# First weights by row block, first squares on GpSimd, a weave's weight and the last scalings: four edits to a two-layer hybrid decoder trunk

## The chip, the cores and the metric

The kernel runs on one core of a Trainium2 chip. The metric is the device time of one launch in microseconds; the median of three runs is the time of a kernel. The engines are named as in the profile: PE is TensorE's matmul side, PEld its weight loads, DVE is VectorE, ACT is ScalarE, POOL is GpSimd, SP is SyncE, which issues the transfers.

## What is computed

Two layers of a decoder, 512 tokens of width 1024, float32, and a closing RMSNorm:

```python
def _layer(x, mem, positions, ...):
    h = _rmsnorm(x, norm_g)
    p = _split_columns(h @ w_in)              # queries, keys, values, gates of all branches
    y_a = _dsa_attention(...)                 # five branches: A sparse, B forgetting (fox),
    y_b = _fox_attention(...)                 # C stick-breaking, D native sparse, E memory
    ...
    merge = jax.nn.sigmoid(p['merge'].reshape(B, S, N_BRANCH, D_MODEL))
    merged = jnp.sum(merge * jnp.einsum('bsnc,ncd->bsnd', ys, w_branch), axis=2)
    return x + merged @ w_out

def reference(x, mem, ...):
    for l in range(2):
        x = _layer(x, ...)
    return _rmsnorm(x, final_norm)
```

## The kernel before

Everything is held transposed: width on the partitions in 8 tiles of 128 rows (index `k`), the 512 tokens along the columns. A weight or an activation is split in a high part, a rounded copy made on ACT, and a low part, the rest, made by a subtraction on DVE; a product is then three matmuls (`mm3`: high by high, high by low, low by high). Weights come in blocks of 128 by 1024 floats: a transfer into one of two buffers `raw`, then a split into one of three `whi` and three `wlo` buffers. Small tiles share 28 slots of 128 by 512 floats (`slot`). PSUM has three banks `pj`, two `S` and three `T`.

The program is written in one order; a scheduler gives each engine its own fixed order from it, by the order of the program and its own estimates of time. Each engine then runs its order strictly and waits where an operand is not there.

**The start.** `begin_layer` and `begin_tile` take the 8 tiles of x: a scaled high part `u` (ACT), the square `sq` (ACT), the low part `ul` (DVE) and the running sum of the squares (DVE). In layer 0 the helper `inorder` chains these instructions on ACT and on DVE in the order in which they are written, and `start_split` puts the splits of the first weights, of `sb_q` and `sb_k` of head pair 0, among them. These weights come in two blocks of 512 KB: the first holds all 8 row tiles of `sb_q`, the second all 8 of `sb_k`. `first` then runs 8 times 2 times 3 matmuls into two banks (`k` outside, query or key inside), sums the squares over the partitions by matmuls with a column of ones (`sumsq`), takes the inverse root on DVE (`rsqrt4`, twelve tiny instructions), spreads it by a transpose (`rowb`), and meanwhile makes the values of `sb_v` from `u` and `ul`. With the spread row `rb`, `norm` makes the normalised activations `h` that every later projection reads.

**The weaves.** `weave` runs several generators in turn: each has a count that grows by 1/n at each step, and the one with the lowest count goes next (at equal counts, the one listed first). The last weave of a layer runs the forgetting attention, 16 steps with n = 16 and a tail behind the last, with the 8 steps of merging branch A, `merge(0, ...)`, n = 8. Behind it `merge(1, ...)` merges branch B, whose operand `yhi`, `ylo` comes out of that tail (inverse sums, `head_rows`, `g`, `y`, split). A merge step is a projection of 24 matmuls from `h` and 6 matmuls from a branch's output.

**The end.** `final` works in two halves of 256 tokens. For each of 8 tiles: 24 matmuls, a residual add (`xn`) on DVE, a square on ACT, an add on DVE. Then `sumsq`, `rsqrt4`, `rowb`, and 8 scalings `o` on DVE straight from PSUM, a store issued from SP for each two of them.

Of the kernel before, what the change touches and what calls it, by code (L numbers as in the profile page):

```python
# [103 lines left out]
def _layout(x, mem, positions, norm_g, w_in, kv_norm, w_uk, w_uv, fox_bias, nsa_pe_k, nsa_pe_v,  # L104
# [6 lines left out]
    for l in range(L):  # L111
        w3 = w_in[l].reshape(KT, 128, -1)

        def cols(idx):
            o = np.zeros((KT, 128, 128), f)
            ok = idx >= 0
            o[:, :, ok] = w3[:, :, idx[ok]]
            return o.transpose(1, 0, 2)

        for a, b in PAIRS:  # L120
            wall[l, CH[a]].reshape(128, 2, KT, 128)[:, 0] = cols(tl[a])
            wall[l, CH[a]].reshape(128, 2, KT, 128)[:, 1] = cols(tl[b])
        for n in VTOK:
# [63 lines left out]
def trunk(ctx: ExitStack, tc: tile.TileContext, xt, memt, pos, wall, small, vec, ca, cb, out):  # L187
# [26 lines left out]

    nc.scalar.preload_act_table_set("exp_and_others")
    xs = big.tile([128, KT, T], F32, name="x0", tag="xa")
    posi = slot("posi", I32)
    VEC = const.tile([128, V_N], F32, name="VEC")
    nc.sync.dma_start(VEC, vec)
    START_W = (1, 3)  # L220
    start_w = []
    for k in range(KT):
        nc.sync.dma_start(xs[:, k], xt[:, k])
        if k in START_W:
            r = wts.tile([128, 1024], F32, name="wraw", tag="raw", bufs=2)
            nc.sync.dma_start(r, wall[0, CH[('sb_q', 0)], :, 1024 * len(start_w):1024 * len(start_w) + 1024])
            start_w.append(r)
    CA = const.tile([128, 896], F32, name="CA")
# [8 lines left out]
    def vcol(c, n=1):  # L237
        return VEC[:, c:c + n]
# [427 lines left out]
    def begin_layer(l):  # L666

        U = [wk.tile([128, 2, T], F32R, name="u", tag=t, bufs=2) for t in ("yhi", "yhi", "ylo", "ylo", "Z", "Z")]
        u = [x[:, e] for x in U for e in range(2)]
        return SimpleNamespace(uh=u[:KT], ul=u[KT:] + [slot("ul", F32R) for _ in range(2 * KT - len(u))], sq=[])  # L670

    def begin_tile(b, l, k, x, inorder=lambda e, ins: ins, middle=lambda k: None):

        sq = slot("sq")
        g = vcol(l * V_L + V_NG + k)
        inorder(0, nc.scalar.activation(b.uh[k], x, AF.Copy, scale=g))
        middle(k)
        inorder(0, nc.scalar.activation(sq, x, AF.Square))
        inorder(1, nc.vector.scalar_tensor_tensor(b.ul[k], x, g, f32(b.uh[k]), op0=OP.mult, op1=OP.subtract))
        if k == 0 or (l and k == KT - 1):  # L680
            b.sq.append(sq)
        else:
            inorder(1, nc.vector.tensor_add(b.sq[0], b.sq[0], sq))

    def layer(l, xs, begin):
# [3 lines left out]
        def first():  # L689
# [4 lines left out]
            if l == 0:  # L694
                prev = {}

                def inorder(e, ins):
                    after(ins, prev.get(e))
                    prev[e] = ins

                def start_split(k):
                    if k in START_W:
                        w = [wts.tile([128, 1024], F32R, name="w", tag=t, bufs=3) for t in ("whi", "wlo")]
                        r = start_w[START_W.index(k)]
                        inorder(0, nc.scalar.activation(w[0], r, AF.Copy))
                        inorder(1, nc.vector.tensor_sub(w[1], r, f32(w[0])))
                        ws.append(w)

                for k in range(KT):
                    begin_tile(b, 0, k, xs[:, k], inorder, start_split)  # L710
                state['start'] = prev[0], prev[1]
            else:
                ws += [wload(l, ('sb_q', 0), 0), wload(l, ('sb_q', 0), 1)]
            uh, ul = b.uh, b.ul
            for k in range(KT):
                for a in range(2):
                    c = slice(128 * k, 128 * k + 128)
                    mm3(p[a], ws[a][0][:, c], ws[a][1][:, c], uh[k], ul[k], k == 0, k == KT - 1)
            y = rsqrt4(sumsq(b.sq, 4), D, 4)
# [590 lines left out]
        def final():  # L1310
# [25 lines left out]
            for half in range(2):  # L1336
                ts = slice(H * half, H * half + H)

                def tiles():
                    for m in range(KT):  # L1340
# [11 lines left out]
                        for k in range(KT):  # L1352
                            c = slice(128 * k, 128 * k + 128)
                            mm3(p, W[m][0][:, c], W[m][1][:, c], lv.g[k][0][:, ts], lv.g[k][1][:, ts], k == 0, k == KT - 1)
                        nc.vector.scalar_tensor_tensor(xn[:, m, ts], p, 0.25, residual(m)[:, ts], op0=OP.mult, op1=OP.add)
                        yield xn[:, m, ts]

                ssq = sumsq(squares(tiles(), True), 2)
                rb = rowb(rsqrt4(ssq, D, 2), 2)
                for j in range(KT // 2):  # L1360
                    o = slot("o", shape=(128, 2, H))
                    for e in range(2):
                        k = 2 * j + e
                        nc.vector.scalar_tensor_tensor(o[:, e], xn[:, k, ts], vcol(V_FIN + k), rb[:, :H], op0=OP.mult, op1=OP.mult)
                    nc.sync.dma_start(out[:, 2 * j:2 * j + 2, ts], o)

# [27 lines left out]
        weave((dsa_attn(), 16), (merge(3, lv.YD), 8), (chain(fox_proj(), silu2('fox_z', lv.ZB)), 7))  # L1394
        weave((fox_attn(), 16), (merge(0, lv.YA), 8))
        run(merge(1, lv.YB, last=True))
# [36 lines left out]
```

## Time and profile before

| | |
|---|---|
| median of 3 runs | 1350.59 us (1350.27 to 1351.06) |
| the profiled execution | 1351.01 us, span 1349.2 us |
| mean granted clock of TensorE | 0.997 |
| busy: PE, PEld | 1310.1 us (97%), 1068.4 us (79%) |
| busy: DVE, ACT, POOL | 892.8 us (66%), 689.0 us (51%), 11.4 us (1%) |

The span is the time from the first to the last event of the profile; the profiled execution took 1.8 us more than its span and 0.42 us more than the median. PE is busy nearly throughout, so what can be won lies where PE waits.

### The profile page before, as it was taken

The page shows a single profiled execution, that of the slowest core. Times are in us where ns is not written, and L with a number is a line of the kernel's source. Part 1 is how long each engine was busy: PE and PEld are TensorE (multiplying, and loading weights), DVE is VectorE, ACT ScalarE, POOL GpSimd, SP SyncE. Part 2 cuts the span into 40 slices and gives each one's busy share as a digit, 9 for nine tenths or more (in the row PEclk, how much of TensorE's full clock was granted, in tenths as well). Part 3 has the DMA queues.
Part 4 walks back from the last instruction along what each step waited for, and adds up shares of the span by engine and source line. Part 5 has one row for each costly group of instructions (what it writes and reads, how often), then busy time and mean ns, then how long its engine had stood idle before and what let it go on. Part 6 is the DMA issues. An engine that isn't in the chain of part 4 may idle for free.

```text
span 1349.2 us, 18962 instructions
## 1 busy us (share of the span) xinstructions
PE 1310.1 (97%) x7240; PEld 1068.4 (79%) x7240; DVE 892.8 (66%) x1847; ACT 689.0 (51%) x1300; POOL 11.4 (1%) x28
## 2 busy tenths in 40 slices
PE   7999999999999999999999999999999999999997
PEld 6777777878888788878887777777788778887896
DVE  6887999767655444545567799995676463454554
ACT  6887834357545434434447795534574452343340
POOL 0000000000000000000000000000000000000000
PEclk9999999999999999999999999999999999999998
DMA  6442321321123132224524313222122222323231
GB/s 215 139 127 77 110 78 63 94 78 59 63 79 102 55 94 78 71 84 130 183 81 126 109 63 110 85 68 84 57 69 63 86 86 66 100 77 103 94 111 63
DMA packets 40235, 124.11 MB, mean 92 GB/s; under 512 B 4432, under 2 KB 6480, under 8 KB 40144
## 3 DMA queue, kind: packets, MB, share of 16 engines
q1 hardware_dynamic: 40144, 122.89, 28.5%
q8 instruction: 57, 0.93, 0.3%
q14 instruction: 34, 0.28, 0.1%
HBM read 118.16 MB, written 4.72 MB: 91 GB/s over the span
## 4 chain that ended last, share of the span: by engine, by line
PE 70%; ACT 6%; DVE 5%; issue 2%; DVEq 0%; ACTq 0%
PE pj L259 58%; PE Y L259 3%; PE S L259 3%; PE pt L556 3%; ACT whi L269 2%; DVE wlo L270 1%; PE hr L621 1%; ACT sw L430 1%; ACT sw L431 1%; PE sbz L259 1%; DVE P L546 0%; ACT P L547 0%; DVE score L902 0%; DVE m L901 0%; ACT Qi L848 0%
## 5 line engine op out<-in xcount | busy, mean ns | idle before, releaser
L259 PE MATMUL pj<-h_hi,whi 128*128 128x512 f32 x1088 | 429.5, 396 | 0.7 <-DVE rt L433 0.7
L259 PE MATMUL pj<-h_hi,wlo 128*128 128x512 f32 x1088 | 429.0, 394 | 0.0
L259 PE MATMUL pj<-h_lo,whi 128*128 128x512 f32 x1088 | 429.0, 394 | 0.0
L270 DVE TENSOR_TENSOR wlo<-wraw,whi 128x1024 fp32r<-128x1024 f32 x183 | 223.7, 1223 | 228.1 <-ACT whi L269 217.0
L269 ACT ACTIVATE whi<-wraw 128x1024 fp32r<-128x1024 f32 x183 | 193.4, 1058 | 319.9 <-PE pj L259 213.9
L259 PEld LDWEIGHTS pj<-h_hi,wlo 128*128 128x128 f32 x1088 | 204.5, 188 | 42.8 <-DVE wlo L270 2.3
L259 PEld LDWEIGHTS pj<-h_hi,whi 128*128 128x128 f32 x1088 | 204.6, 188 | 40.5 <-issue 1.7
L259 PEld LDWEIGHTS pj<-h_lo,whi 128*128 128x128 f32 x1088 | 204.6, 188 | 40.4 <-issue 1.8
L547 ACT ACTIVATE P<-P,nm 128x128 f32<-128x128 f32 (+3 forms) x128 | 71.6, 559 | 67.7 <-DVE nm L546 64.2
L259 PE MATMUL pj<-yhi,whi 128*128 128x512 f32 (+1 forms) x192 | 71.9, 374 | 2.9 <-ACT yhi L269 2.9
L259 PE MATMUL pj<-yhi,wlo 128*128 128x512 f32 (+1 forms) x192 | 71.6, 373 | 0.0
L259 PE MATMUL pj<-ylo,whi 128*128 128x512 f32 (+1 forms) x192 | 71.5, 372 | 0.0
L556 PE MATMUL pt<-CA,P 128*128 128x128 f32 x384 | 62.7, 277 | 2.6 <-ACT P L1274 1.3
L546 DVE CUSTOM_DVE_ANT_0 P<-S,CA 128x128 f32<-128x128 f32 (+3 forms) x104 | 47.6, 468 | 18.1 <-PE S L259 18.0
L556 PEld LDWEIGHTS pt<-CA,P 128*128 128x128 f32 x384 | 44.9, 141 | 18.2 <-ACT P L1274 6.0
L259 PE MATMUL S<-Ks,Qs 128*128 128x256 f32 (+2 forms) x160 | 51.0, 358 | 6.6 <-DVE nm L546 6.5
L394 ACT ACTIVATE G<-pj 128x512 f32<-128x512 f32 x92 | 53.6, 582 | 0.3
L902 DVE MATCH_REPLACE8 score<-m,score 128x256 f32<-128x256 f32 (+2 forms) x96 | 51.7, 541 | 0.0
L901 DVE MAX8 m<-score 128x8 f32<-128x256 f32 (+2 forms) x96 | 49.7, 546 | 0.0
L799 DVE SCALAR_TENSOR_TENSOR G<-G,pj 128x512 f32<-128x512 f32 x64 | 43.6, 681 | 3.6 <-PE pj L259 3.3
L800 DVE TENSOR_TENSOR acc<-acc,G 128x512 f32<-128x512 f32 x64 | 44.0, 688 | 0.9
L259 PEld LDWEIGHTS pj<-yhi,whi 128*128 128x128 f32 x192 | 36.2, 188 | 10.4 <-ACT yhi L269 4.0
(478 smaller groups left out, 2006.1 us busy)
## 6 DMA issues: line engine op xcount, KB each, us to landing
wraw<-in_wall_dram SPq DMA_DIRECT2D x192, 512.0 KB, 3.7
wc<-in_wall_dram SPq DMA_DIRECT2D x16, 256.0 KB, 6.1
x<-in_xt_dram SPq DMA_DIRECT2D x8, 256.0 KB, 7.0
mraw<-in_memt_dram SPq DMA_DIRECT2D x4, 512.0 KB, 4.7
xo<-in_xt_dram SPq DMA_DIRECT2D x8, 256.0 KB, 4.3
xspill<-xn SPq DMA_DIRECT2D x8, 256.0 KB, 2.2
xo<-xspill SPq DMA_DIRECT2D x8, 256.0 KB, 4.0
out_dram<-o SPq DMA_DIRECT2D x8, 256.0 KB, 2.2
```

What stands on the lines that cost most here:

```text
L259: return nc.tensor.matmul(out_, lhsT, rhs, start=start, stop=stop, **kw)
L269: nc.scalar.activation(hi, raw, AF.Copy)
L270: nc.vector.tensor_sub(lo, raw, hi.bitcast(F32))
L394: i = nc.scalar.activation(*a, **k)
L430: nc.scalar.activation(sw[a], p[b], AF.Copy)
L546: nc.vector.tensor_tensor_reduce(P, S, mask, -1.0, 3e38, OP.add, OP.min, nm)
L547: nc.scalar.activation(P, P, AF.Exp, bias=nm, scale=-1.0, accum_out=sums)
L556: nc.tensor.transpose(pt[:, 128 * j:128 * j + 128], x[:, c:c + 128], ident)
L799: nc.vector.scalar_tensor_tensor(G, G, gc, p, op0=gop, op1=OP.mult)
L800: nc.vector.tensor_add(acc, acc, G)
L901: nc.vector.max(m8, lv.work[i])
L902: nc.vector.match_replace(lv.work[i], m8, lv.work[i], REPL)
```

## The change

- The first weights are laid out by row block: 256 columns for each `k`, query and key side by side, loaded as four blocks of 256 KB (two `k` each) in the order of use. The first block and the small constants `VEC` are issued from ACT, ahead of its table load; the rest from SP between the tiles of x. Each block is split as it comes, in front of the two tiles that it is multiplied with. `first` reads them in that layout in both layers.
- In layer 0 the squares of tiles 0 to 3 and their sum move to GpSimd (4 products, 3 adds); those of tiles 4 to 7 are made on ACT behind the last `u` and summed on DVE. `sumsq` then takes two tiles.
- The last weave of each layer runs `merge(0, ...)` with 6 in place of 8.
- In `final`, tiles 6 and 7 of each half are scaled by their gain on GpSimd as they come, `rb` is copied out of PSUM by ACT, and GpSimd multiplies the two; their store is issued from ACT. DVE scales the other six.

```diff
         for a, b in PAIRS:
-            wall[l, CH[a]].reshape(128, 2, KT, 128)[:, 0] = cols(tl[a])
-            wall[l, CH[a]].reshape(128, 2, KT, 128)[:, 1] = cols(tl[b])
+            w2 = wall[l, CH[a]].reshape(128, 2, KT, 128)
+            if a == ('sb_q', 0):
+                w2 = wall[l, CH[a]].reshape(128, KT, 2, 128).transpose(0, 2, 1, 3)
+            w2[:, 0] = cols(tl[a])
+            w2[:, 1] = cols(tl[b])
...
-    nc.scalar.preload_act_table_set("exp_and_others")
...
-    nc.sync.dma_start(VEC, vec)
-    START_W = (1, 3)
-    start_w = []
-    for k in range(KT):
-        nc.sync.dma_start(xs[:, k], xt[:, k])
-        if k in START_W:
-            r = wts.tile([128, 1024], F32, name="wraw", tag="raw", bufs=2)
-            nc.sync.dma_start(r, wall[0, CH[('sb_q', 0)], :, 1024 * len(start_w):1024 * len(start_w) + 1024])
-            start_w.append(r)
+    start_w = [wts.tile([128, 1024], F32, name="wraw", tag="raw", bufs=2) for _ in range(2)]
+
+    def start_load(k):
+        c = slice(512 * (k % 4) // 2, 512 * (k % 4) // 2 + 512)
+        nc.scalar.dma_start(start_w[k // 4][:, c], wall[0, CH[('sb_q', 0)], :, 256 * k:256 * k + 512])
+
+    start_load(0)
+    nc.sync.dma_start(xs[:, 0], xt[:, 0])
+    nc.scalar.dma_start(VEC, vec)
+    nc.sync.dma_start(xs[:, 1], xt[:, 1])
+    nc.scalar.preload_act_table_set("exp_and_others")
+    for k in range(2, KT, 2):
+        c = slice(512 * (k % 4) // 2, 512 * (k % 4) // 2 + 512)
+        nc.sync.dma_start(start_w[k // 4][:, c], wall[0, CH[('sb_q', 0)], :, 256 * k:256 * k + 512])
+        for e in range(2):
+            nc.sync.dma_start(xs[:, k + e], xt[:, k + e])
...
         g = vcol(l * V_L + V_NG + k)
+        middle(k)
         inorder(0, nc.scalar.activation(b.uh[k], x, AF.Copy, scale=g))
-        middle(k)
+        inorder(1, nc.vector.scalar_tensor_tensor(b.ul[k], x, g, f32(b.uh[k]), op0=OP.mult, op1=OP.subtract))
+        if l == 0:
+
+            if k < 4:
+                nc.gpsimd.tensor_mul(sq, x, x)
+                if k:
+                    nc.gpsimd.tensor_add(b.sq[0], b.sq[0], sq)
+                else:
+                    b.sq.append(sq)
+            else:
+                b.rest.append((x, sq))
+            return
         inorder(0, nc.scalar.activation(sq, x, AF.Square))
-        inorder(1, nc.vector.scalar_tensor_tensor(b.ul[k], x, g, f32(b.uh[k]), op0=OP.mult, op1=OP.subtract))
-        if k == 0 or (l and k == KT - 1):
+        if k == 0 or k == KT - 1:
             b.sq.append(sq)
...
+                ws += [[wts.tile([128, 1024], F32R, name="w", tag=t, bufs=3) for t in ("whi", "wlo")] for _ in range(2)]
+
                 def start_split(k):
-                    if k in START_W:
...
+                    if k % 2 == 0:
+                        c = slice(256 * (k % 4), 256 * (k % 4) + 512)
+                        hi, lo = (x[:, c] for x in ws[k // 4])
+                        r = start_w[k // 4][:, c]
+                        inorder(0, nc.scalar.activation(hi, r, AF.Copy))
+                        inorder(1, nc.vector.tensor_sub(lo, r, f32(hi)))
 
                 for k in range(KT):
                     begin_tile(b, 0, k, xs[:, k], inorder, start_split)
+                for k, (x, sq) in enumerate(b.rest):
+                    inorder(0, nc.scalar.activation(sq, x, AF.Square))
+                    if k:
+                        inorder(1, nc.vector.tensor_add(b.rest[0][1], b.rest[0][1], sq))
+                b.sq.append(b.rest[0][1])
                 state['start'] = prev[0], prev[1]
...
-                    c = slice(128 * k, 128 * k + 128)
-                    mm3(p[a], ws[a][0][:, c], ws[a][1][:, c], uh[k], ul[k], k == 0, k == KT - 1)
+                    c = slice(256 * (k % 4) + 128 * a, 256 * (k % 4) + 128 * a + 128)
+                    mm3(p[a], ws[k // 4][0][:, c], ws[k // 4][1][:, c], uh[k], ul[k], k == 0, k == KT - 1)
...
                         nc.vector.scalar_tensor_tensor(xn[:, m, ts], p, 0.25, residual(m)[:, ts], op0=OP.mult, op1=OP.add)
+                        if m >= KT - 2:
+                            s = slot("xg")[:, :H]
+                            nc.gpsimd.tensor_scalar(s, xn[:, m, ts], vcol(V_FIN + m), None, op0=OP.mult)
+                            scaled.append(s)
                         yield xn[:, m, ts]
 
                 ssq = sumsq(squares(tiles(), True), 2)
                 rb = rowb(rsqrt4(ssq, D, 2), 2)
-                for j in range(KT // 2):
+                rs = rows_sb(rb, H, "rb")
+                for j in (3, 0, 1, 2):
                     o = slot("o", shape=(128, 2, H))
                     for e in range(2):
                         k = 2 * j + e
-                        nc.vector.scalar_tensor_tensor(o[:, e], xn[:, k, ts], vcol(V_FIN + k), rb[:, :H], op0=OP.mult, op1=OP.mult)
-                    nc.sync.dma_start(out[:, 2 * j:2 * j + 2, ts], o)
+                        if j == 3:
+                            nc.gpsimd.tensor_mul(o[:, e], scaled[e], rs)
+                        else:
+                            nc.vector.scalar_tensor_tensor(o[:, e], xn[:, k, ts], vcol(V_FIN + k), rb[:, :H], op0=OP.mult, op1=OP.mult)
+                    (nc.scalar if j == 3 else nc.sync).dma_start(out[:, 2 * j:2 * j + 2, ts], o)
...
-        weave((fox_attn(), 16), (merge(0, lv.YA), 8))
+        weave((fox_attn(), 16), (merge(0, lv.YA), 6))
```

## Rows read from the trace of the kernel before

**Rows 1.** The page: busy time, share of the span and instructions of each engine.

```profile
PE 1310.1 (97%) x7240; PEld 1068.4 (79%) x7240; DVE 892.8 (66%) x1847; ACT 689.0 (51%) x1300; POOL 11.4 (1%) x28
```

**Rows 2.** PE's waits in the whole span: for whom, us in total, times, longest.

```profile
PE pj L259 <- ACT w L705: 9.8, 1, 9.8
...
PE pj L259 <- ACT yhi L269: 2.9, 3, 1.3
```

**Rows 3.** Timeline of the start, SP, ACT and PE: start, duration, instruction, [idle before <- releaser].

```profile
0.74 0.40 SPq L219 DMA_DIRECT2D VEC<-in_vec_dram  x1
...
8.70 1.06 ACT L705 ACTIVATE w<-wraw 128x1024 fp32r<-128x1024 f32 x1 [2.49 <-DMA wraw<-in_wall_dram]
...
9.81 9.26 PE L259 MATMUL pj<-u,w 128*128 128x512 f32 x25 [9.81 <-ACT w L705]
10.18 0.71 ACT L676 ACTIVATE u<-x,VEC 128x512 fp32r<-128x512 f32 x1
10.79 0.61 ACT L678 ACTIVATE sq<-x 128x512 f32<-128x512 f32 x1
```

**Rows 4.** Tile view of x, start: its transfers' issues (duration; first and last start) and landings.

```profile
L223 SPq DMA_DIRECT2D x<-in_xt_dram x8: 412/455/1154, 1.2 to 6.8; - x8
...
DMA to landing us min/median/max: 3.1/7.0/7.5
```

**Rows 5.** Timeline of the start, DVE and PE.

```profile
10.93 0.75 DVE L679 SCALAR_TENSOR_TENSOR u<-x,VEC,u 128x512 fp32r<-128x512 f32 x1
11.59 0.69 DVE L683 TENSOR_TENSOR sq<-sq 128x512 f32<-128x512 f32 x1
12.19 0.75 DVE L679 SCALAR_TENSOR_TENSOR u<-x,VEC,u 128x512 fp32r<-128x512 f32 x1
...
20.32 0.68 DVE L683 TENSOR_TENSOR sq<-sq 128x512 f32<-128x512 f32 x1
20.92 0.42 DVE L359 TENSOR_SCALAR k<-ang 128x512 f32<-128x512 f32 x1
...
24.12 0.95 PE L259 MATMUL ssq<-ones,sq 128*128 128x1 f32 x8
...
25.10 0.16 DVE L297 TENSOR_SCALAR rs_v<-ssq 128x4 f32<-128x4 f32 x1 [1.56 <-PE ssq L259]
```

**Rows 6.** POOL's instructions of the whole span by shape: count, busy us, mean ns.

```profile
L476 POOL MEMSET Ks<- 64x512 f32 x16 | 8.7, 545 | 932.5 <-PE S L259 389.8 <-DVE sq L683 386.7 <-issue 61.1
L476 POOL MEMSET KlE<- 64x256 f32 x8 | 2.4, 306 | 15.2 <-ACT sq L336 8.4 <-DVE h_lo L270 6.5
```

**Rows 7.** Timeline of POOL in the start.

```profile
12.34 0.52 POOL L476 MEMSET Ks<- 64x512 f32 x1 [11.89 <-DVE sq L683]
```

**Rows 8.** PE's timeline behind the last weave, layer 0, then layer 1.

```profile
577.84 0.40 PE L259 MATMUL pj<-h_hi,wlo 128*128 128x512 f32 x1
579.51 0.49 PE L259 MATMUL pj<-yhi,whi 128*128 128x512 f32 x1 [1.27 <-ACT yhi L269]
...
1239.27 0.40 PE L259 MATMUL pj<-h_hi,wlo 128*128 128x512 f32 x1
1240.94 0.50 PE L259 MATMUL pj<-yhi,whi 128*128 128x512 f32 x1 [1.27 <-ACT yhi L269]
```

**Rows 9.** Busy us (x instructions) by stretch: PE, PEld, DVE, ACT, POOL, clock, DMA, GB/s.

```profile
520.00:540.00 20.00, 20.00 (x101) 16.23 (x100) 10.54 (x28) 10.27 (x23) 0.00 (x0) 1.00 0.25 79
...
590.00:600.00 10.00, 10.00 (x46) 8.29 (x45) 4.01 (x6) 2.81 (x4) 0.00 (x0) 1.00 0.31 102
```

**Rows 10.** Timeline of the end, DVE and SP.

```profile
1342.99 3.22 DVE L1364 SCALAR_TENSOR_TENSOR o<-xn,VEC,rowb 128x256 f32<-128x256 f32 x8 [0.85 <-PE rowb L317]
...
1345.46 1.16 SPq L1365 DMA_DIRECT2D out_dram<-o  x2
```

**Rows 11.** Tile view of `o`, from 1310 us: shortest, median and longest scaling, then its stores' landings.

```profile
L1364 DVE SCALAR_TENSOR_TENSOR o<-xn,VEC,rowb x16: 472/475/481, 1318.8 to 1345.7; 128x256 f32<-128x256 f32 x16
...
DMA to landing us min/median/max: 2.1/2.2/2.2
```

More of the change, by code (lines that the diff above doesn't have):

```diff
@@ L669, in begin_layer @@
         u = [x[:, e] for x in U for e in range(2)]
-        return SimpleNamespace(uh=u[:KT], ul=u[KT:] + [slot("ul", F32R) for _ in range(2 * KT - len(u))], sq=[])
+        return SimpleNamespace(uh=u[:KT], ul=u[KT:] + [slot("ul", F32R) for _ in range(2 * KT - len(u))], sq=[], rest=[])
     def begin_tile(b, l, k, x, inorder=lambda e, ins: ins, middle=lambda k: None):
@@ L699, in inorder @@
                     prev[e] = ins
+                ws += [[wts.tile([128, 1024], F32R, name="w", tag=t, bufs=3) for t in ("whi", "wlo")] for _ in range(2)]
                 def start_split(k):
-                    if k in START_W:
[L703 to L707, printed above, removed]
+                    if k % 2 == 0:
[4 more added lines that the diff above has]
+                        inorder(1, nc.vector.tensor_sub(lo, r, f32(hi)))
                 for k in range(KT):
                     begin_tile(b, 0, k, xs[:, k], inorder, start_split)
+                for k, (x, sq) in enumerate(b.rest):
[3 more added lines that the diff above has]
+                b.sq.append(b.rest[0][1])
                 state['start'] = prev[0], prev[1]
@@ L1337, in final @@
                 ts = slice(H * half, H * half + H)
+                scaled = []
                 def tiles():
```

## Prediction

> **What bounds the kernel now.** I read the busy shares first: PE is busy 97% of the span and no other engine over 79% [rows 1]. So only time in which PE waits can be won. The list of PE's waits names two that the change touches: 9.8 us before the first matmul, which waits for the split of the first weights, and 2.9 us, in three waits, for `yhi` [rows 2]. The third place is the end, where PE has finished and DVE and the stores run alone [rows 10].
>
> The timeline of the start shows the chain: ACT waits 2.49 us for the first weight block and splits it at 8.70, PE starts at 9.81 [rows 3]. Both blocks are needed for `k` = 0, so PE stutters until the second one is split too. DVE's chain of `ul` and sums ends at 20.32 + 0.68 = 21.0; it does 2.6 us of other work, waits 1.56 us, and takes the row sums at 25.10 [rows 5]. That is the marker of the start: the inverse root, `rb` and all of `norm` hang on it.
>
> **The weights by row block, and the squares.** The bytes on the way to the last tile of x stay what they were; SP has 11 issues up to it as before, ACT two. Both queues start at 0.74, and x starts in the place where `VEC` was, 0.46 us earlier (1.20 less 0.74 [rows 3, 4]). ACT's two issues and its table load are done long before the first data.
>
> The first x landed 3.1 us after its issue, at 4.3; the last was issued at 6.8 and took 7.5, so 14.3 [rows 4]. Now the first tile shares the line with the first 256 KB of weights. I take 4.7 for both (an estimate: 4.3, less 0.46, and some 0.9 for the second 256 KB, as (14.3 - 4.3) / 11 for each of the 11 pieces of that size which follow the first tile), and 14.3 - 0.46 = 13.8 for the last tile. ACT then splits 512 columns and makes `u`, 0.6 and 0.7 [rows 3]: PE starts at 6.0, not 9.8.
>
> PE's work is 48 matmuls; a stretch with nothing else in it shows 46 in 10 us, 0.22 each [rows 9], so 10.6 us and an end near 17 to 18, where the old order ended at 24.12 [rows 5].
>
> What DVE does decides whether that can be used. Its chain becomes 4 splits, 8 `ul` and 3 adds, where it was 2 long splits, 8 `ul` and 7 adds. From start to start an `ul` takes 0.66 and an add or a split of 512 columns 0.60 [rows 5]. GpSimd takes 4 products and 3 adds of 128x512. Nothing like these is in the trace: POOL only runs memsets, 0.306 us for 256 columns and 0.545 for 512, that is 0.93 ns a column [rows 6]. Lower bound: one such pass, 0.55. Upper bound: each operand read and the result written in turn, three passes, 1.5. I take 1.0, two passes, between them.
>
> The open question is whether GpSimd delays DVE. A DVE instruction with one operand takes 0.42 for 512 columns, one with two operands 0.69 [rows 5]: the first moves two columns at a time, so the engine has two reading paths and the second form fills both. Whether GpSimd reads through one of them no row shows, as its memsets read nothing; one of them ran from 12.34 beside an `ul` from 12.19, which took 0.75 like the one at 10.93 [rows 5, 7]. I take it as likelier that a reading GpSimd instruction and a two-operand DVE instruction take turns: all of DVE's chain has two operands, and no third path shows anywhere.
>
> The Trainium skill says the same and more sharply, on its page "SBUF — State Buffer", section "Who interferes with whom": a DVE instruction with two SBUF inputs contends with a GpSimd instruction that reads SBUF, not with one that only writes, and the second to come waits for all of the first. The memset row agrees with its second half; no run here shows the first. Its "GPSIMD Engine Reference", section "Performance versus the Vector engine", has 4497 ns for an add of 2048 floats, so by my estimate from it 1.12 us for 512; with that price the marker below would fall at 25.2 and the total 0.8 us higher.
>
> Turns, by rows: from 4.7 on, the first seven DVE instructions (3 splits of 0.69, 4 `ul` of 0.75: 5.1 us) alternate with seven of POOL (7.0 us), and the other eight follow in their usual steps (4 x 0.66 + 4 x 0.60 = 5.0). The chain ends at 4.7 + 5.1 + 7.0 + 5.0 = 21.8; the 2.6 us of other work take it to 24.4, against 25.10: **0.7 us won**. PE isn't late there: its last products need only the last `ul`, 1.8 us before the chain's end, and 6 matmuls behind it. `sumsq` has 16 passes instead of 8 (8 took 0.95 [rows 5], so about 1.7) and is through at 23.5. Their cover is the same DVE work; without it they would cost 0.8. The second buffer `raw` is free for the next weights (`sb_v`) when the last block is split, 4.7 + 5.1 + 7.0 + 2 x 0.66 + 0.6 = 18.7; a landing of 7.0, as the tiles of x had in the full queue [rows 4], makes that 25.7, about when the value products come to this half, so I charge nothing; late, it is the next wait. Bounds: at 0.55 a POOL instruction the marker is at 21.2 (3.9 won), at 1.5 at 27.9 (2.8 lost).
>
> In the second layer nothing is earned: its first products run behind the out projection with no PE wait of theirs in the list [rows 2].
>
> **The last weave.** Behind it PE stands from 577.84 to 579.51, 1.67 us for a step of 0.23, and as long at 1239.27 in the other layer, both for `yhi` [rows 8]: 2 x 1.44 = 2.9 us. With n = 6 the counts of `merge(0)` grow by 1/6. Six of them add up to a hair under 1, so the seventh step still goes ahead of the tail and only the eighth stays behind it. One step is 30 matmuls, 6.6 us of PE work between the tail and the first product with `yhi`; 1.44 us are to be hidden. Cost inside the weave: one step less to fill the gaps of 16. There PE is busy 20.00 of 20 us while DVE and ACT have 10.54 and 10.27 [rows 9], so I charge 0.1 us for both layers (bounds 0 and 1). **2.8 us won**, bounds 1.9 and 2.9.
>
> **The end.** Eight scalings run in 3.22 us, the last 0.48 long, so one each 0.39 [rows 10, 11]. Two fewer bring the last store from SP forward by **0.8 us**. GpSimd's way must be shorter than DVE's 6 x 0.39 + 0.1 = 2.4 us: a copy of `rb` on ACT (under 0.6, the 512 columns of a square [rows 3]) and two products of 256 columns, at 1.0 / 2 each: 1.6 us, and the store from ACT goes out before SP's last. At the upper bound, 0.75 each, it is 2.1 and still hidden. DVE's scalings read PSUM and one SBUF tile, so they don't take turns with it by the argument above. Bounds 0.3 and 0.8. In the first half all this lies beside PE's second half: ACT's store waits there some 2 us for GpSimd, and the squares queued behind it feed a sum that nobody reads before that half ends. Without that cover it would cost the 2 us.
>
> **Sum.** 0.7 + 2.8 + 0.8 = 4.3 us. The profiled execution of 1351.01 would become 1346.7; it stands 0.42 above the median, so against the median of 1350.59 I forecast **1346.3**.
>
> **The rivals.**
>
> *GpSimd costs DVE nothing* (chance 0.33). For it: a memset beside DVE delays nothing. Against: it reads nothing. Then the last x, 13.8, sets the pace: `u` 0.6, four squares 2.4 on ACT, the last add 0.7, DVE's chain ends at 17.5 and the marker falls at 20.1, 5.0 us won. Total 8.6: 1342.0. The page of the skill named above speaks against this one.
>
> *Turns, as forecast* (0.45): 1346.3, by the bounds of the POOL instruction 1343 to 1350.
>
> *The weave's edit does not do what it says* (0.12): the scheduler has its own order, and PE may meet a wait for `yhi` or for a head's scores elsewhere. With turns that leaves 0.7 + 0.8: 1349.1.
>
> *Slower* (0.06): the same place, GpSimd in the start, at a higher price. The start must lose more than the 3.6 us of the other two parts, so the marker would have to pass 28.7, and the seven instructions take over 11.3 us: from 1.6 us each on, just past my upper bound, the kernel is slower than before. At 2.0 each it is 1353. What speaks for it: DVE's sums would wait and PE with them. Against: no pass of 512 columns in these rows takes over 0.75.
>
> The remaining 0.04 is for order changes elsewhere, as the scheduler lays out everything anew.
>
> **Range and chances.** From 1341.0 to 1349.5 holds the first rival nearly whole, the forecast but for a GpSimd instruction above 1.4 us, and the third: some 0.82. A difference under 0.2%, 2.7 us, can't be told from no change here. Faster than that, under 1347.9: the first rival, and of the forecast the part with a GpSimd instruction under 1.2 us (0.33): 0.67 with the rest. Within 0.2%: 0.25. Slower: 0.08.
>
> **What would show it.** In the start of the changed profile: the first matmul near 6.0; DVE's `ul` of tiles 0 to 3 pushed apart by about 1 us each or longer than 0.75 (turns), or close together (no turns); POOL's products near 1.0 us; the row sums taken at 24.4 (turns) or 20.1. Behind the weaves: no wait of PE for `yhi`. At the end: six scalings and ACT's store issued before SP's last. The prediction is wrong if the first transfers land later than 4.7 with two queues, if GpSimd is much slower, or if a new wait appears in the weaves.

## The result, and the profile after

The changed kernel takes 1358.3 us (median of 4 runs, 1357.35 to 1358.55), the kernel before 1350.43 beside it: a ratio of 1.006 (95% interval 1.0042 to 1.0077), 8 us slower. The forecast was 1346.3, with a range up to 1349.5: wrong, on the other side. The profiled execution took 1358.2 us with a span of 1356.4, 7.2 longer than before.

PE's waits in the whole span (for whom; us in total, times, longest), to be read beside [rows 2]:

```profile
PE pj L269 <- ACT u L687: 8.5, 1, 8.5
...
PE ssq L269 <- DVE sq L352: 2.7, 1, 2.7
...
PE pj L269 <- DVE Qs L468: 2.3, 1, 2.3
...
PE pj L269 <- DVE w L758: 1.2, 1, 1.2
...
PE pj L269 <- DVE ul L688: 0.7, 1, 0.7
...
PE pj L269 <- ACT yhi L279: 0.4, 1, 0.4
```

The first wait is 1.3 us shorter, those for `yhi` fell from 2.9 to 0.4. Four new ones, 6.9 us together, stand in the first 63 us: for `ul`, for the split of `sb_v` (`w` L758), for the squares of the memory rows (`ssq`), and for `Qs`. The memory rows (`memory_rows`) are the squares, sums and inverse root of `mem`, which scale the memory branch; these `Qs` are the stacked queries of the second head pair of branch C (`sb`), and `VE` holds the values of the memory branch. The matmuls of the later stages confirm the place: the first product with `VE` comes at 168.71 us against 160.79, so 7.9 us are lost by then. The end costs 1.0 more (from the last `ssq` to the end of the span 11.0 us against 10.0), and the weaves give 1.7 back.

The start, timelines of ACT, POOL, DVE, PE and SP (start, duration, instruction, [idle before <- releaser]):

```profile
1.17 0.46 ACTq L230 DMA_DIRECT2D VEC<-in_vec_dram  x1
...
7.70 1.34 ACT L687 ACTIVATE u<-x,VEC 128x512 fp32r<-128x512 f32 x2 [1.61 <-DMA VEC<-in_vec_dram]
...
5.21 1.04 POOL L692 TENSOR_TENSOR sq<-x 128x512 f32<-128x512 f32 x1 [4.78 <-DMA x<-in_xt_dram]
...
9.21 1.56 POOL L692 TENSOR_TENSOR sq<-x 128x512 f32<-128x512 f32 x1 [0.65 <-DMA x<-in_xt_dram]
10.73 1.74 POOL L694 TENSOR_TENSOR sq<-sq 128x512 f32<-128x512 f32 x1
...
8.46 1.41 DVE L688 SCALAR_TENSOR_TENSOR u<-x,VEC,u 128x512 fp32r<-128x512 f32 x2 [1.64 <-ACT u L687]
...
11.24 3.23 DVE L688 SCALAR_TENSOR_TENSOR u<-x,VEC,u 128x512 fp32r<-128x512 f32 x2
...
20.39 2.27 DVE L737 TENSOR_TENSOR sq<-sq 128x512 f32<-128x512 f32 x3
...
24.93 0.16 DVE L307 TENSOR_SCALAR rs_v<-ssq 128x4 f32<-128x4 f32 x1 [1.94 <-PE ssq L269]
...
25.41 1.22 DVE L758 TENSOR_TENSOR w<-wraw,w 128x1024 fp32r<-128x1024 f32 x1
...
8.48 8.73 PE L269 MATMUL pj<-u,w 128*128 128x512 f32 x26 [8.48 <-ACT u L687]
...
26.69 2.33 PE L269 MATMUL pj<-w,u 128*128 128x256 f32 x11 [1.21 <-DVE w L758]
...
19.16 13.85 SPq L288 DMA_DIRECT2D wraw<-in_wall_dram  x4
```

The first `u` has its weights split at 6.1 but waits until 7.70 for `VEC`, issued behind the first weights. A GpSimd product alone takes 1.04 us; beside DVE the products take 1.50 and 1.56 and the sums 1.72 to 1.74 (no sum ran alone), and two `u` of DVE take 3.23 instead of 1.41. DVE's chain ends at 22.66 (20.39 + 2.27). It then waits 1.94 us for `ssq`, so here PE sets the row sums. The split of `sb_v` stands behind the row sums on DVE and PE waits for it.

The memory rows: DVE and PE before, then after. These rows of the kernel before are new; they are its timeline from 54 to 60 us:

```profile
54.10 1.48 DVE L342 TENSOR_TENSOR sq<-sq 128x256 f32<-128x256 f32 x3
...
56.81 0.95 DVE L342 TENSOR_TENSOR sq<-sq 128x256 f32<-128x256 f32 x2
58.27 0.68 DVE L458 SCALAR_TENSOR_TENSOR Qs<-pj,Qs 64x512 fp32r<-64x512 f32 x1 [0.50 <-ACT Qs L465]
...
59.92 0.60 PE L259 MATMUL ssq<-ones,sq 128*128 128x1 f32 x4 [0.36 <-DVE sq L342]
```

```profile
55.43 3.06 DVE L352 TENSOR_TENSOR sq<-sq 128x256 f32<-128x256 f32 x6
58.52 0.68 DVE L468 SCALAR_TENSOR_TENSOR Qs<-pj,Qs 64x512 fp32r<-64x512 f32 x1
59.24 0.42 DVE L352 TENSOR_TENSOR sq<-sq 128x256 f32<-128x256 f32 x1
...
60.44 1.23 DVE L280 TENSOR_TENSOR wlo<-wraw,whi 128x1024 fp32r<-128x1024 f32 x1
...
61.78 0.69 DVE L468 SCALAR_TENSOR_TENSOR Qs<-pj,Qs 64x512 fp32r<-64x512 f32 x1
...
59.72 0.61 PE L269 MATMUL ssq<-ones,sq 128*128 128x1 f32 x4 [2.69 <-DVE sq L352]
62.62 0.76 PE L269 MATMUL pj<-h_hi,whi 128*128 128x512 f32 x1 [2.29 <-DVE Qs L468]
```

Nobody edited this place. But the scheduler now has six of the seven sums in a row ahead of the first `Qs`, and the matmuls `ssq` some 22 places sooner on PE, ahead of the projection that could have filled the time. The second `Qs`, for which PE waits 2.29, stands behind the row sums, which need `ssq`, and behind a weight split of 1.23. SP's order changed as well: the four transfers of the memory rows go out together from 42.83 and the next weights at 53.98; before, two of them went at 40.05, the weights at 50.44 and the other two from 50.81. The windows (busy us of PE, PEld, DVE, ACT, POOL; granted clock; DMA share; GB/s) show what followed; before, PE had 9.64 and 10.00 of these two stretches, at 1.00:

```profile
50.00:60.00 10.00, 7.31 (x35) 5.65 (x33) 8.57 (x16) 9.83 (x20) 1.90 (x6) 1.00 0.40 126
60.00:70.00 10.00, 7.71 (x28) 5.85 (x29) 6.64 (x22) 5.59 (x16) 0.00 (x0) 0.66 0.35 113
```

From 58 to 62 us PE is busy for 0.61 us; from 62 to 68 the granted clock is 0.50, the lower of its two levels (1.2 of 2.4 GHz). Twelve products of 512 columns start 0.43 us apart there instead of 0.23: by this estimate some 2.4 us more, on top of the waits.

The end, ACT, DVE and SP, beside [rows 10], and the landings of the stores, beside [rows 11]:

```profile
1349.23 0.38 ACT L357 ACTIVATE rb<-rowb 128x256 f32<-128x256 f32 x1 [3.87 <-PE rowb L327]
...
1349.72 2.44 DVE L1401 SCALAR_TENSOR_TENSOR o<-xn,VEC,rowb 128x256 f32<-128x256 f32 x6 [1.34 <-ACT rb L357]
...
1350.62 1.94 SPq L1402 DMA_DIRECT2D out_dram<-o  x3
...
DMA to landing us min/median/max: 2.3/2.9/3.0
```

DVE waits 1.34 us where it waited 0.85, now for ACT's copy (from the end of the transposition to the first scaling 0.53 instead of 0.03), and every store lands later than the 2.2 of before.

### The profile page after: what moved, and what is told of

Its sections match the earlier page's. It is cut to its first block, busy times and chain, and to the rows that moved or that the text cites. A ratio compares the mean times of both kernels' runs of the same rounds, so it can differ in the third digit from the quotient of the medians.

```text
span 1356.4 us, 19012 instructions
## 1 busy us (share of the span) xinstructions
PE 1314.5 (97%) x7248; PEld 1071.6 (79%) x7248; DVE 893.5 (66%) x1841; ACT 688.5 (51%) x1300; POOL 28.0 (2%) x43
## 4 chain that ended last, share of the span: by engine, by line
PE 68%; ACT 7%; DVE 6%; issue 2%; DMA 1%; DVEq 0%; ACTq 0%
PE pj L269 56%; PE Y L269 3%; PE S L269 3%; PE pt L566 3%; ACT whi L279 2%; DVE wlo L280 1%; PE hr L631 1%; ACT sw L440 1%; ACT sw L441 1%; DMA mraw<-in_memt_dram 1%; ACT P L557 1%; DVE P L556 0%; PE sbz L269 0%; DVE score L930 0%; DVE m L929 0%
## 5 line engine op out<-in xcount | busy, mean ns | idle before, releaser
L566 PEld LDWEIGHTS pt<-CA,P 128*128 128x128 f32 x384 | 44.8, 141 | 18.7 <-ACT P L1302 6.2
L269 PEld LDWEIGHTS S<-Ks,Qs 128*128 128x128 f32 x160 | 28.4, 189 | 17.3 <-DVE nm L556 15.0
```

What stands on the lines that cost most here:

```text
L269: return nc.tensor.matmul(out_, lhsT, rhs, start=start, stop=stop, **kw)
L566: nc.tensor.transpose(pt[:, 128 * j:128 * j + 128], x[:, c:c + 128], ident)
```

## The experiments

Theory A after the result: the loss is made in the first 70 us. Rival B: the weave's edit re-orders work and loses there. First each part alone on the kernel before, and the changed kernel without GpSimd's squares.

**The start alone, the weave alone, the end alone.** `e1_start` keeps the old end and `merge(0, lv.YA), 8`; `e2_weave` is one number; `e3_end` is the last two hunks of `final`.

> The kernel before with only the new start (row blocks, squares on GpSimd); the last weave keeps 8 steps and the end is the old one. Theory A (the loss is made in the first 70 us): the time is about 8 us above the kernel before, as the changed kernel's first matmul with Y reached its place 7.9 us later than before, and nothing behind the start gives any of it back; 1358 to 1359. Rival B (the weave's edit re-orders work elsewhere and loses there): the start alone costs under 3 us, 1353 or less, and the rest of the 7.2 us appears in the second kernel of this set.

> The kernel before with only 6 in place of 8 in the last weave. Theory A: the two waits for yhi go, but the last step that is moved ahead takes 0.4 to 0.7 us of PE time that was hidden elsewhere; gain 1.7 us as the anchors of the two traces show (0.7 and 1.0), 1348.8. The forecast's own term: 2.8 us, 1347.7. Rival B (it re-orders work elsewhere): no gain or a loss, 1350.5 or more.

> The kernel before with only the new end: two products on GpSimd, the copy of rb on ACT, stores on two queues. Theory A: DVE's first scaling waits for ACT's copy of the same PSUM bank, as it did in the changed kernel (1.34 us between it and its predecessor against 0.03 before), and the four stores land later; +0.9 us, 1351.4. Rival (that wait came only from the changed start or from the order in that kernel): the scalings start right behind the row sums as before and the end is 0.8 us shorter, 1349.8.

Measured: 1359.61 (ratio 1.007, 1.0056 to 1.0084), 1349.12 (0.9989, 0.998 to 0.9998) and 1351.16 (1.0008, 0.9999 to 1.0017). Theory A holds: +9.5, -1.5 and +1.1 us, the last at the edge of what can be told (`e1_start` is 0.6 above the expected 1359). Rival B is out. The expectation of `e3_end` sets a wait of 1.34 against 0.03; the wait of before was 0.85, and the 0.03 is counted from the end of the transposition.

**No GpSimd in the start.** The first layer's branch in `begin_tile` and the second loop over `b.rest` go:

```diff
-        if l == 0:
-            if k < 4:
-                nc.gpsimd.tensor_mul(sq, x, x)
...
-        if k == 0 or k == KT - 1:
+        if k == 0 or (l and k == KT - 1):
```

> The changed kernel, but the squares of the first layer are made on ACT and summed on DVE, all in one chain, as before the change; the row blocks stay. Theory A (GpSimd and DVE take turns and this holds up the second buffer and with it the value weights): the DVE instructions of the start go back to 0.69 and 0.6 from start to start, the second weight buffer comes free some 3 us earlier, PE does not lose 1.2 us and its clock at 27 us; some 3 to 5 us come back, 1353.5 to 1355.5. Rival C (the row blocks themselves and the late VEC are what costs): 1357 to 1359, the first matmul still at 8.5. Rival D (what costs is the order that the scheduler chose between 30 and 70 us, which follows from no single wait): anything, and the ten microseconds from 50 to 60 tell: PE busy 7.3 as in the changed kernel or 9.6 as before.

Measured 1355.69 (1.0044, 1.0031 to 1.0058): 2.2 us by the ratios, 2.6 by the medians come back, no more. DVE's steps are 0.60 to 0.67 again and the value products end at 35.9, as in the kernels with the old start (36.95 in the profile of before, 35.1 to 36.2 in five others). Still the time is nearly 6 us above before, with waits of 2.47 for `ssq` and 2.29 for `Qs`, and PE at 5.24 of 10 us from 50 to 60. So most of the loss was rival D's: an order. That became theory A2.

**The order, undone and done.** A first try swapped two generators, in the changed kernel, in the one without GpSimd squares, and with `VEC` first on SP and the old end besides:

```diff
-            run(chain(memory_rows(), take(sp1, 1)))
+            run(chain(take(sp1, 1), memory_rows()))
```

> The changed kernel whole, with one line of the program swapped: the projections of the second sb pair are written ahead of the memory rows' squares and sums. In the order that follows, DVE makes both Qs ahead of the seven sums, and PE takes the matmuls ssq 28 places later. Theory A2 (some 5 to 6.5 us of the loss is this order alone: in the changed kernel PE stood 2.7 us for ssq and 2.3 us for Qs at 57 to 63 us and then ran at the lower granted clock): 1358.4 less 5 to 6.5, so 1352 to 1353.5, and what is left above the kernel before is the start's own 2.8 us and the end's 1 us less the weave's 1.7. Rival (the order is a symptom: the start is late, and PE meets the lateness elsewhere): 1356 or more, with a wait of the same size at another place.

> The changed kernel with the squares back on ACT and DVE (row blocks kept) and the same swapped line. Theory A2: the run without GpSimd squares stood at 1355.7 with its end of the value products 0.9 us earlier than in the kernel before; without the 2.5 and 2.3 us waits and the clock behind them it falls by 5 to 6.5, to 1349.2 to 1350.7. Rival: 1354 or more.

> As the one before, and besides the first transfer from SP is VEC again, ahead of x, and the end is the old one; the weave's 6 stays. Theory A2: against the kernel before it wins 1.5 us in the weaves, 0.9 or more in the start, and loses nothing at the end: 1347.0 to 1348.5. If the late VEC was what held PE at 8.5 us (the first u waited 1.4 to 1.6 us for it), the first matmul comes at 7.1 or sooner. Rival (the row blocks cost something that stays): 1349 or more.

Measured: 1365.63, 1362.95 and 1360.63 (ratios 1.0112, 1.0092, 1.0074). All three lie 12 to 14 us above what theory A2 expected, and where the rivals put them (1356, 1354 and 1349 or more). PE's timeline of `f1_swap` shows part of the reason:

```profile
66.88 0.61 PE L269 MATMUL ssq<-ones,sq 128*128 128x1 f32 x4 [2.91 <-DVE sq L352]
88.99 0.39 PE L269 MATMUL pj<-yhi,whi 128*128 128x256 f32 x1 [1.30 <-ACT whi L279]
90.25 0.39 PE L269 MATMUL pj<-yhi,wlo 128*128 128x256 f32 x1 [0.76 <-DVE wlo L280]
```

The wait for `Qs` is gone, but `ssq` still waits 2.91, 7 us later, as the rival said; PE waits 2.6 for `sp` of the `sb` branch behind it, and the products of the memory branch now stand for their weights (`mraw` and the weights share the two `raw` buffers; that this is the cause was not tried alone). The swap moved one wait and added others, so by itself it didn't decide between theory A2 and its rival. `f3_best` showed one thing more: with `VEC` first, PE starts at 6.2.

The order was then made in the kernel before, whose start is unchanged, by one dependence (`left` counts the weight transfers written behind the memory rows):

```diff
+            if state.get('left', 0):
+                state['left'] -= 1
+                if not state['left']:
+                    after(i, state['memdma'])
```

> The kernel before, its start, weave and end unchanged, with one dependence more: the fourth weight transfer written behind the memory rows' transfers is issued behind all four of them. The scheduler then lays the matmuls ssq of the memory rows 21 places sooner on PE, right behind the scores, and six of the sums ahead of Qs on DVE, nearly as in the changed kernel. Theory A2 (this order costs 5 to 6.5 us by itself): 1355 to 1356.5, with waits of PE for ssq and Qs near 55 us and the lower granted clock behind them. Rival (the order costs only because the changed start is late): 1352 or less.

Measured 1354.97 (1.0035, 1.0024 to 1.0046): +4.7 us with the start, the weave and the end of before. PE's timeline and the window:

```profile
55.99 1.00 PE L259 MATMUL ssq<-ones,sq 128*128 128x1 f32 x4 [2.32 <-DVE sq L346]
```

```profile
50.00:60.00 10.00, 7.35 (x27) 5.48 (x26) 7.08 (x14) 9.12 (x20) 1.23 (x4) 0.80 0.05 12
```

Of the two expected waits only that for `ssq` came. The clock is 0.50 or 0.51 from 56 to 62 us, for eleven products of 512 columns: some 2.2 us by the estimate above, as much as the wait itself. The dependence moved transfers too (the memory rows' from 30.80, the next weights at 58.36 instead of 50.44), and PE waits 0.33 for those weights; so the price is that of the whole new order, SP's included.

The other direction, in the changed kernel whole: a `yield` behind the fourth square, and the other half written behind the projections.

```diff
+            if k == 4:
+                yield
...
-            run(chain(memory_rows(), take(sp1, 1)))
+            mr = memory_rows()
+            run(chain(take(mr, 1), take(sp1, 1), mr))
```

> The changed kernel whole, with the memory rows written in two halves around the projections of the second sb pair, so that the sums are spread between the Qs as in the kernel before, and ssq stands 16 places later on PE. Theory A2 (place of ssq and Qs costs, and the swap failed because it put all seven sums and what hangs on them behind everything): PE waits under 2 us for ssq and not for Qs, the first product with VE comes at 164.5 to 166 instead of 168.7, time 1354 to 1356. Rival (in this kernel any order loses here, since its start is late by 3 us): 1357.5 or more.

Measured 1353.63 (1.0027, 1.0016 to 1.0039), 4.7 us under the changed kernel: no wait for `ssq`, 1.68 left for `Qs` (none was expected), the first product with `VE` at 164.18.

```profile
58.12 0.47 PE L269 MATMUL pj<-h_hi,whi 128*128 128x512 f32 x1 [1.68 <-DVE Qs L478]
```

By the medians both directions give the same price. That they agree so well is partly chance: in the two profiles 1.46 of the 4.53 us by the first product with `VE` stand already at the end of the value products (39.73 against 38.27), where the changed kernel ran at the lower clock from 28 to 30 us and `g2_split` did not. That the order alone can cost much shows twice more: `f1_swap` and `g2_split` differ in nothing but where the memory rows are written, and so do `f3_best` and `g3_cand` below; each pair lies 11 to 12 us apart.

**The start taken apart, in that order of the memory rows.** `g3_cand` has the row blocks, `VEC` first on SP, squares on ACT and DVE, the weave's 6 and the old end. `h2_pool` adds the GpSimd squares to it, `h3_latevec` the changed kernel's place of `VEC`, `h1_tab` writes `run(tabg)` behind the splits of `sb_v`, `h4_cand2` cuts the memory rows behind the second square besides.

> Row blocks, VEC first on SP, squares on ACT and DVE, the weave's 6, the old end, and the memory rows in two halves as in the run beside it. Theory A2: no long wait for ssq, first matmul at 6.2, value products done at 34.2 against 36 to 37 before, the first product with VE at 160 to 161.5, 1348.5 to 1350. If the order of before was itself a lucky one, which no writing of the memory rows in this place reaches, the time stays at 1351 or more whatever the start wins.

> The run g3_cand with the changed kernel's GpSimd squares (four products, three sums) in the first layer, the order of the memory rows unchanged. Theory T (turns; the forecast's mechanism, but its price was set against a marker that DVE's other work hid, and PE waits for the split of sb_v): DVE's chain of the start ends 2 to 3 us later than in g3_cand, the value products end 2.4 to 3 us later than 34.6, 1351 to 1352. Rival (GpSimd was harmless, and the loss against the run without it came from the order alone): 1349 to 1349.5, value products at 34.6.

> The run g3_cand with VEC issued from ACT behind the first weights, as in the changed kernel. Theory V (the forecast had no term for VEC: its 128 rows of 492 bytes land at 7.7 us behind 256 KB in the same transfer engines, and every u waits for it): first matmul at 8.3 to 8.6 instead of 6.7, the chain of the start 1.2 to 1.6 us later, 1350 to 1350.6. Rival (the pace is set by the last x, so a late start of PE is caught up): the value products end at 34.6 as in g3_cand, 1349.

> The run g3_cand with one move: the rotary tables' arithmetic is written behind the splits of sb_v, so that DVE splits the first half of sb_v right behind the last sum, at about 19 us, instead of at 21.8. There PE waited 1.5 us for it. Theory S (the scheduler's place of this split is what PE waited for, not the late buffer): that wait goes, the value products end 1 to 1.5 us sooner than 34.6, and the time falls by up to 1.2 us, to 1347.7 to 1348.5. Rival (the second half of sb_v is the next wait, since its buffer comes free only at 16.4 us): the wait moves to the second half and the time stays at 1349.

> As h1_tab, and the memory rows are cut behind the second square instead of the fourth, so that both Qs stand ahead of all sums but the first on DVE. In g3_cand PE waited 1.5 us for Qs near 58 us. Theory A2: that wait falls under 0.5 us, and ssq, 3 places later on PE, is in time; 1 us less than h1_tab, 1346.7 to 1347.7. Rival: ssq or what hangs on the memory rows waits instead, as in the swap; no less than h1_tab.

| kernel | median us | ratio to before | 95% interval |
|---|---|---|---|
| `g3_cand` | 1348.94 | 0.9992 | 0.9983 to 1.0001 |
| `h2_pool` | 1352.84 | 1.0021 | 1.0011 to 1.003 |
| `h3_latevec` | 1350.73 | 1.0004 | 0.9995 to 1.0013 |
| `h1_tab` | 1348.31 | 0.9985 | 0.9976 to 0.9993 |
| `h4_cand2` | 1346.05 | 0.9971 | 0.9961 to 0.9982 |

GpSimd's squares cost 3.9 us, a little more than theory T's 1351 to 1352; its rival is out. DVE and PE in `h2_pool`:

```profile
6.40 2.26 DVE L698 SCALAR_TENSOR_TENSOR u<-x,VEC,u 128x512 fp32r<-128x512 f32 x2 [0.65 <-ACT u L697]
...
23.97 0.16 DVE L307 TENSOR_SCALAR rs_v<-ssq 128x4 f32<-128x4 f32 x1 [1.48 <-PE ssq L269]
...
16.38 0.50 PE L269 MATMUL pj<-ul,w 128*128 128x512 f32 x1 [1.24 <-DVE ul L698]
...
22.09 1.84 PE L269 MATMUL ssq<-ones,sq 128*128 128x1 f32 x16
...
25.72 1.58 PE L269 MATMUL pj<-w,u 128*128 128x256 f32 x11 [1.21 <-DVE w L768]
...
37.28 0.39 PE L269 MATMUL pj<-h_hi,whi 128*128 128x512 f32 x1
```

And PE in `g3_cand`:

```profile
20.08 0.95 PE L269 MATMUL ssq<-ones,sq 128*128 128x1 f32 x8
...
23.08 1.58 PE L269 MATMUL pj<-w,u 128*128 128x256 f32 x11 [1.47 <-DVE w L752]
...
34.64 0.40 PE L269 MATMUL pj<-h_hi,whi 128*128 128x512 f32 x1
```

The row sums are taken at 23.97, sooner than the 25.10 of before, and the value products still end at 37.3 against 34.6 in `g3_cand`. The wait for the split of `sb_v` is no part of this: `g3_cand` has it too, 1.47 against 1.21. What differs is that PE comes to `ssq` 2.0 us later, with waits of 1.24 and 0.28 for `ul`, and that the 16 matmuls `ssq` take 1.70 us to the next product where 8 took 0.81. By the first product with `VE` the difference is 3.8 us (163.43 against 159.64); the last 1.15 of it come behind the value products and are not taken apart. The late `VEC` costs 1.8 us by the medians, first matmul at 8.43 against 6.73; the two intervals overlap, so its size is not sharp. The value products end at 37.2 in the profile of `h3_latevec`, so a late start of PE is not caught up; but that profile is of the slowest of its runs (1353.1). Moving the tables (theory S) takes away the wait of 1.47 for `w` that `g3_cand` had, and the value products end at 33.5; the time falls by 0.6, within the intervals. With both `Qs` ahead of the sums PE's wait for them is 0.39 instead of the 1.46 of `g3_cand` (1.0 in `h1_tab`), nothing waits for `ssq`, and `h4_cand2` is 4 us faster than the kernel before: the best of all, and below what was expected. PE's timeline there:

```profile
6.24 8.94 PE L269 MATMUL pj<-u,w 128*128 128x512 f32 x25 [6.24 <-ACT u L697]
...
52.14 0.47 PE L269 MATMUL pj<-h_hi,whi 128*128 128x512 f32 x1 [0.39 <-DVE Qs L478]
```

**The end.** `g1_bank` is `e3_end` with `rs = rows_sb(rowb(y, 2), H, "rb")`, a second transposition; `g4_store` is `e2_weave` with the first store cut in two.

> The kernel before with only the new end, but ACT copies its rb from a second transposition in another PSUM bank, so that DVE's first scaling has no wait for ACT. Theory E1 (that wait is what cost at the end, 0.38 of copy and the handing on): the first scaling starts 0.5 us sooner after the transposition than in the run with the new end alone, and the first store with it. Theory E2 (the end is set by 1 MB of stores that move at 335 to 345 GB/s, 3.1 us, from the first store on, so that only the first store counts and not the last scaling): even so nothing is won against the kernel before, 1349.5 to 1350.5, from the first transposition to the end of the span 6.9 to 7.1 us as before; by E1 alone, with two scalings fewer, it would be 6.1 and 1349.3 or less.

> The kernel before with the weave's 6 and one edit at the end: the first store is cut in two, one tile each, so that the stores begin one scaling (0.4 us) sooner; nothing else changes. Theory E2: 0.3 to 0.4 us less than the weave's edit alone, 1348.5 to 1349, and from the transposition to the end of the span 6.5 us instead of 6.9. Theory E1 or the forecast's view (the last scaling and the last store set the end): no change from the weave's edit alone, or up to 0.5 us lost by the one issue more on SP.

Measured: 1351.82 (1.0007, 0.9998 to 1.0016) and 1348.8 (0.9988, 0.9979 to 0.9996; `e2_weave` had 0.9989). In `g1_bank` DVE's wait is 0.67 instead of 1.34:

```profile
1341.61 2.44 DVE L1374 SCALAR_TENSOR_TENSOR o<-xn,VEC,rowb 128x256 f32<-128x256 f32 x6 [0.67 <-PE rowb L317]
```

From the last `ssq` to the end of the span it has 9.8 us, `e2_weave` 10.1, `e3_end` 10.5, `g4_store` 10.3. The wait of E1 is real, but taking it away did not show in the time: `g1_bank` is above both expectations, 1349.5 to 1350.5 by E2 and 1349.3 or less by E1. Theory E2 fails in `g4_store` as well: it expected 6.5 us from the transposition to the end of the span, and there are 7.2, against 7.0 in `e2_weave`. The DMA view of 1340 to 1349 us (40 slices, GB/s) shows one stream in `e2_weave`, and one with a hole in `g4_store`:

```profile
GB/s 0 0 0 0 0 0 0 0 0 0 0 0 27 309 350 309 310 350 323 332 337 341 319 328 355 350 301 18 0 0 0 0 0 0 0 0 0 0 0 0
```

```profile
GB/s 0 0 0 0 0 0 155 350 173 360 128 32 323 350 300 301 360 332 323 351 337 346 141 0 0 0 0 0 0 0 0 0 0 0 0 0 0 0 0 0
```

At some 335 GB/s a store of 256 KB takes 0.78 us, as long as its two scalings (2 x 0.39). Stores and scalings keep the same pace: starting the stores sooner wins nothing while the last scaling stays (`g4_store`), and fewer scalings win nothing in the time either (`g1_bank`). Both together were not tried.

## Why the prediction was wrong

A chain of kernels, each with one thing more, gives the account, by the ratios times 1350: weave's 6, -1.5; row blocks with `VEC` first and the memory rows in two halves, +0.4; GpSimd's squares, +3.9; the late `VEC` with the new end, +0.8; the order of the memory rows, +4.5. Together 8.1 us. By the intervals each step is uncertain by 1.2 to 2.8 us, so the +0.4 and the +0.8 can't be told from nothing, and a step's size depends on what was there already (the squares cost 2.2 in `e4_nopool`'s comparison).

**The step that failed most: "order changes elsewhere", 0.04, without a price.** It is 4.5 to 4.7 us of 8, shown in both directions, waits and lower clock together. The edits shift the scheduler's own estimates, and it laid the memory rows' sums in one piece ahead of `Qs`. That it might do so stood in the text; that PE can come to wait twice around 55 us, for `ssq` and for `Qs`, when DVE's sums stand in one row was not looked for, though [rows 2] covers the whole span and the timeline of before had the 0.36 for `ssq`. The rival "slower" would have hit the sign only: it needed more than 11.3 us in the seven GpSimd instructions, and they took 10.3.

**The start: the mechanism was right, the marker was wrong.** Turns: yes. GpSimd at 1.04 alone (forecast 1.0), DVE's chain at 22.66 (forecast 21.8, in `h2_pool` 22.15), the row sums at 24.93 and 23.97 (24.4). That the row sums came so near is luck: the chain was to be followed by 2.6 us of other work, but DVE did 0.42 of it and waited 1.94 and 1.48 for PE's `ssq`. The Trainium skill has the rule on its page "SBUF — State Buffer", section "Who interferes with whom", and by the rows above it agrees: both engines' instructions grow when they overlap. But the gain was read off the row sums, and "PE isn't late there" failed: in `h2_pool` PE waits 1.24 and 0.28 for `ul` and does 8 more matmuls `ssq`, and it is PE's own work, value products and all behind them, that sets the end. The forecast had put the 8 matmuls (0.8) under DVE's other work; on PE nothing covers them, and they cost 0.9. DVE's chain ends there at 22.15, in `g3_cand` at 18.25 + 0.68 = 18.93; of those 3.2 us PE pays 2.0 by its `ssq`, although the row sums come sooner than in the kernel before. So the start's 0.7 won became some 4 lost, 3.9 of it by the squares. What the row blocks alone win stays open: in `g3_cand` the waits for the split of `sb_v` and for `Qs` stand against it, and without them `h4_cand2` is 2.4 us below `e2_weave` by the ratios.

**First data at 4.7, PE at 6.0.** With `VEC` first, PE starts at 6.2 to 6.7, as forecast (the kernel before, unchanged there, started at 8.5 to 9.8 in the profiles of the runs). In the changed kernel it is 8.5: the step counted ACT's issue of `VEC` and not its landing, 6.5 us later behind the weights. Beside GpSimd this is nearly hidden (0.8 together with the new end).

**The second `raw` buffer** was free at 19.1 (forecast 18.7), charged with nothing, and not what PE waited for: it was the split of the first half of `sb_v`, written early and placed late on DVE.

**The weave: right, mis-sized.** The waits for `yhi` go. The way from the last group of products with `VA` to the first of the out projection shrank in `e2_weave` by 0.66 us in layer 0 (126.21 to 125.55), not by 1.44: PE's idle 1.27 is gone, but the same matmuls take 0.6 us longer in the new order. In layer 1 it shrank by 1.16 (126.95 to 125.79). The charge inside the weave was 0.1 for both layers and measured 1.1 by these ways, 1.4 by the time; the total is 1.5 us (0.3 to 2.7) instead of 2.8.

**The end: failed.** 0.8 us won became 1.0 lost in the changed kernel. GpSimd's way is hidden, as forecast: its products end at 1351.17, DVE's scalings at 1352.16. One cause is shown, DVE's wait for ACT's read of the same PSUM bank, which the forecast's "reads PSUM and one SBUF tile" passed over. The Trainium skill states on its page "PSUM — Partial Sum Buffer", section "PSUM bank collisions raise a hardware error", that two engines' accesses to one bank must be kept apart, reads too; the wait of 1.34 with one bank and 0.67 with two agrees. The other is the stores' own pace. Which of them carries how much of the 1.0 stays open.

## What to carry to other kernels

Where a scheduler lays out the order from its own estimates, an edit in one place can cost most in another: look in the trace of before for the stretches in which one engine's row of work has two waiters, and pin that order before trying the edit. Measure a gain at the engine that is busy 97% of the time, not at a marker on another engine. A move to another queue is priced by when its data land, and by who else reads what it reads.

## What the runs showed that was not expected

The same wait of 1.21 us near 26 us was followed by the lower level of the granted clock in the changed kernel (0.50 from 28 to 30 us, 1.2 of 2.4 GHz) and neither in `g2_split` nor in `e1_start` (1.00 from 20 to 30); what decides it no run here tells. The time around the span is fixed for a kernel, 1.8 us in eleven of the sixteen and 2.0 to 2.4 in `e1_start`, `e3_end`, `f2_np_swap`, `g1_bank` and `h2_pool`, so about half a microsecond of the loss of `e3_end` and `g1_bank` lies outside their spans; its cause is open.
